# Moving the weights and block sums of a two-layer encoder to multiples of 128 bytes in SBUF

## The chip, the cores and the metric

The kernel runs on one core of one Trainium2 chip. The metric is device time in microseconds from launch to end, as the median of several runs. One execution is also recorded by the hardware profiler; its "page" and the answers of its trace are what this document reads. Engines carry their short names: PE is TensorE's matmul stream, PEld its weight loads, DVE VectorE, ACT ScalarE, POOL GpSimd, SP the engine that issues most transfers.

## The reference

One sequence of 512 frames with 1024 features goes through two layers. Everything is float32.

```python
def reference(x, ...):
    h = x
    for layer in range(2):
        if layer < 1:
            mix = hgrn2_mixer(rms_norm(h, a_norm_pre[0]), a_w_in[0], ...)   # gated recurrence, 8 heads
            h = h + rms_norm(mix, a_norm_post[0])
        else:
            mix = diff_attn_mixer(rms_norm(h, b_norm_pre[0]), k_sh, v_sh, ...)  # 8 heads, two softmaxes each
            h = h + rms_norm(mix, b_norm_post[0])
        ff = squared_relu_mlp(rms_norm(h, mlp_norm_pre[layer]), w_up[layer], w_down[layer])
        h = h + rms_norm(ff, mlp_norm_post[layer])
        if layer == 0:
            k_sh, v_sh = shared_kv(h, kv_norm, w_kv)
    return h
```

Nearly all of the arithmetic is in the projections: the recurrence's input and output projections, the key, value and query projections, the attention's output projection, and in each layer an MLP of 1024 to 4096 to 1024 features.

## The kernel before

**Products in three parts.** TensorE multiplies float32 operands in the type `float32r`, which keeps fewer digits. To keep precision, every operand of a projection is split into a high and a low part: `hi` is the value rounded to float32r, `lo` the rest. A product is then three matmuls (`mm3`, line 224): high by high, high by low, low by high. The high part is written by ScalarE, the low part by VectorE (`split_w` line 166, `split_b` line 195, `split_d` line 185; the activations at lines 389 and 390, 474 and 475).

**Two operands of a matmul.** The stationary operand, 128 by 128, is loaded into the array beforehand (a row LDWEIGHTS on PEld); the moving operand streams through in 128, 256 or 512 columns (a row MATMUL on PE). In `wmm` (line 229) the weights are stationary and the activations moving; in `xmm` (line 235) it is the other way round. All matmuls are issued by the `pe` helper at line 114, so groups of matmuls are told apart by the names of their tiles.

**Tiles.** Activations live feature-major in `xhi` and `xlo` (normed input of a projection) and `uhi` and `ulo` (hidden units or mixer output), four tiles of [128, 2, 512] each, made first, at lines 122 to 127. Weights are fetched in 512 KB pieces into four `raw` buffers by the SP queue (`fetch_w`, line 155) and split into eight `whi` and eight `wlo` buffers in the pool `wp`. The order on TensorE is written out by the program (`Plan`, line 45, with due times); the other engines follow the order in which the program emits, save for chains that get a higher priority.

**Block products.** Quarters 1 to 3 of each MLP's up-projection (`Pair`, line 503) and parts of the gate and value projections (`gates_pair` line 933, `values_pairs` line 974) use seven products of half-size blocks in place of eight. They multiply block sums of the weights (`whi_s`, `whi_t` and their low parts) by block sums of the activations: tiles `t` in the block stage, made by `sums_x` at line 481, and `whi_x` and `wlo_x` in the recurrence, made by `block_sums` at line 702. The accumulators are `ux`, `uy` and `uz`. One product is 12 matmuls of 256 columns. Some of the seven take `t` as the moving operand, the others `xhi` and `xlo`.

**Names in the rows.** `qf`, `g`, `i`: the recurrence's query and forget, gate, and value projections. `ao` and `bo` with `_h` or `_last`: the two mixers' output projections. `up`, `dn`, `dn_h`, `dn_last`: plain up-projection and down-projection. `kq` and `v`: key with query, and value, of the attention. `lg`: attention logits.

**Where tiles start.** The allocator places tiles of the pool `cp` in the order in which they are made, each in a slot rounded up to 32 bytes; `wp` follows, then the pools of the stages (`hg`, `mlp0`, `at`, `mlp1`). `gn` holds 82 gains per partition, 328 bytes, and so takes 352; the same holds for `gnh` (line 144). The addresses of the kernel before, in bytes within a partition:

| tiles | first address | modulo 128 | modulo 512 |
|---|---|---|---|
| xhi, xlo, uhi, ulo (4096 each) | 16512 | 0 | 128 |
| gn (328) | 82048 | 0 | 128 |
| ident, mask, onesd, ones1 | 82400 | 96 | |
| rb (2048) | 84384 | 32 | |
| gnh (328) | 86496 | 96 | |
| raw, whi, wlo (4096 each) | 87488 | 64 | 448 |
| zacc, rs, ss, t, r, u and all other large tiles of the stages | 169408 | 64 | |
| attention's kq, l, at | 192192 | 64 | 192 |

Slices that matmuls take out of x, u, weight and block-sum tiles start at multiples of 512 bytes within the tile, so a row of this table holds for all its slices.

Of the kernel before, what the change touches and what calls it, by code (L numbers as in the profile page):

```python
# [9 lines left out]
F32 = mybir.dt.float32  # L10
# [7 lines left out]
P = 128  # L18
# [23 lines left out]
G_N = 82  # L42
# [46 lines left out]
def trunk_kernel(ctx: ExitStack, tc: tile.TileContext, x_t, w_qf, w_g, w_gs, w_i, w_is, w_ao, w_kv, w_q, w_bo, w_up, w_us, w_dn,  # L89
# [3 lines left out]
    cp = ctx.enter_context(tc.tile_pool(name="cp", bufs=1))  # L93
# [33 lines left out]
    ulo = [cp.tile([P, 2, S], F32R, tag=f"ulo{i}", name=f"ulo{i}", bufs=1) for i in range(4)]  # L127

    res = [x_t.rearrange("(k p) t -> p k t", p=P)[:, :, lo:hi] for lo, hi in ((0, 256), (256, 512))]
    gn = cp.tile([P, G_N], F32, name="gn")  # L130
    a.dma_start(gn, gains)
    ident = cp.tile([P, P], F32, name="ident")
    mask = cp.tile([P, len(LEVELS), 64], U8, name="mask")
# [7 lines left out]
    rcol = cp.tile([P, 4], F32, name="rcol")  # L141
    nrcol = cp.tile([P, 4], F32, name="nrcol")
    ea = rb
    gnh = cp.tile([P, G_N], F32, name="gnh")
    v.tensor_scalar(gnh, gn, -0.5, None, op0=ALU.mult)
    epsc = cp.tile([P, 1], F32, name="epsc")
    v.memset(epsc, EPS)
# [1220 lines left out]
```

## Time and profile before

| | us |
|---|---|
| median of 3 runs | 1262.08 (1261.12 to 1263.5) |
| the profiled execution | 1259.98 |
| its span, first to last instruction | 1258.1 |
| PE busy | 1234.5 |
| PEld busy | 1119.2 |
| DVE busy | 828.9 |
| ACT busy | 669.9 |
| POOL busy | 96.0 |

The mean granted clock of TensorE was 0.997. Matmuls are pipelined: a row's duration runs from a matmul's start to its modelled end and overlaps the next one, so busy time says that TensorE had work, not how fast it went. The chain of work that ended last goes back from the last instruction, step by step, to what released it; its pieces in order of time have a start, a length, an engine, the tile written and the number of instructions merged. By stage: the recurrence layer's mixer runs to about 305 us, its MLP to 652, the attention to about 850 with its output projection to about 900, the second MLP to the end.

### The profile page before, as it was taken

How to read it: one execution, taken by the hardware profiler on the slowest of the kernel's cores; microseconds unless marked ns; L12 is line 12 of the kernel's file. 1: busy time of each engine (PE TensorE's matmuls, PEld its weight loads, DVE VectorE, ACT ScalarE, POOL GpSimd, SP SyncE). 2: the span in 40 equal slices, each digit the busy share in tenths (PEclk: the TensorE clock that was granted, in tenths of full speed). 3: DMA queues.
4: the chain of work that ended last, by engine and by line, in shares of the span. 5: the costliest groups of instructions: out<-in, count | busy, mean ns of one | idle time of the engine just before them, and what ended most of it. 6: DMA issues, size and time to landing. Idle time of an engine off the chain costs nothing.

```text
span 1258.1 us, 21436 instructions
## 1 busy us (share of the span) xinstructions
PE 1234.5 (98%) x8440; PEld 1119.2 (89%) x8440; DVE 828.9 (66%) x1649; ACT 669.9 (53%) x1244; POOL 96.0 (8%) x174
## 2 busy tenths in 40 slices
PE   9999999999999999999999999999999999999996
PEld 7889899999988989989999788889998898988996
DVE  6878887867854735636498978564785473663645
ACT  6454545437742724616456877664773371561732
POOL 0202211110000000000100000001000000000000
PEclk9999999999999999999999999999999999999998
DMA  7224544244366564635526322222435365463522
GB/s 255 90 51 116 112 109 122 88 152 137 105 160 130 169 142 109 182 86 145 191 78 192 115 88 84 85 81 88 152 111 150 93 180 120 114 188 77 162 98 67
DMA packets 56726, 156.44 MB, mean 124 GB/s; under 512 B 6289, under 2 KB 8594, under 8 KB 56626
## 3 DMA queue, kind: packets, MB, share of 16 engines
q1 hardware_dynamic: 45920, 120.34, 30.4%
q0 software_dynamic: 10464, 34.61, 13.0%
q8 instruction: 66, 1.08, 0.3%
q14 instruction: 34, 0.28, 0.1%
q10 hardware_dynamic: 242, 0.13, 0.0%
HBM read 145.35 MB, written 9.70 MB: 123 GB/s over the span
## 4 chain that ended last, share of the span: by engine, by line
PE 87%; DVE 5%; ACT 3%; DMA 3%; issue 2%; POOL 0%; SPq 0%; DVEq 0%; ACTq 0%
PE dn L114 21%; PE ux L114 9%; PE up L114 7%; PE qf L114 7%; PE kq L114 6%; PE dn_h L114 5%; PE uz L114 4%; PE bo_h L114 3%; PE ao_h L114 3%; PE gl L114 3%; PE v L114 2%; PE g L114 2%; PE uy L114 2%; PE i L114 2%; PE lg L114 2%
## 5 line engine op out<-in xcount | busy, mean ns | idle before, releaser
L114 PE MATMUL dn<-uhi,whi_dn 128*128 128x512 f32 x384 | 152.0, 396 | 0.0
L114 PE MATMUL dn<-uhi,wlo_dn 128*128 128x512 f32 x384 | 151.9, 396 | 0.0
L114 PE MATMUL dn<-ulo,whi_dn 128*128 128x512 f32 x384 | 151.8, 395 | 0.0
L114 PEld LDWEIGHTS dn<-uhi,whi_dn 128*128 128x128 f32 x384 | 72.2, 188 | 17.8 <-ACT r L570 0.7
L200 ACT ACTIVATE whi_a<-raw_a 128x1024 fp32r<-128x1024 f32 x24 | 25.4, 1058 | 117.5 <-PE dn L114 114.0
L114 PEld LDWEIGHTS dn<-uhi,wlo_dn 128*128 128x128 f32 x384 | 72.2, 188 | 17.4
L114 PEld LDWEIGHTS dn<-ulo,whi_dn 128*128 128x128 f32 x384 | 72.2, 188 | 16.8
L173 DVE TENSOR_TENSOR wlo_dn<-raw_dn,whi_dn 128x1024 fp32r<-128x1024 f32 x64 | 76.6, 1220 | 5.9 <-ACT whi_dn L172 4.6
L475 DVE TENSOR_TENSOR ulo<-r,uhi 128x1024 fp32r<-128x1024 f32 (+1 forms) x40 | 40.2, 1010 | 53.9 <-ACT uhi L474 53.9
L114 PE MATMUL up<-xhi,wlo_up 128*128 128x256 f32 x256 | 72.1, 281 | 1.0 <-DVE wlo_up L173 1.0
L114 PE MATMUL up<-xhi,whi_up 128*128 128x256 f32 x256 | 72.6, 284 | 0.0
L114 PE MATMUL up<-xlo,whi_up 128*128 128x256 f32 x256 | 71.8, 281 | 0.0
L172 ACT ACTIVATE whi_dn<-raw_dn 128x1024 fp32r<-128x1024 f32 x64 | 65.7, 1051 | 7.2 <-PE up L114 3.0
L114 PE MATMUL dn_h<-uhi,whi_dn 128*128 128x256 f32 x240 | 66.6, 278 | 0.0
L114 PE MATMUL dn_h<-uhi,wlo_dn 128*128 128x256 f32 x240 | 66.3, 276 | 0.0
L114 PE MATMUL dn_h<-ulo,whi_dn 128*128 128x256 f32 x240 | 66.3, 276 | 0.0
L617 DVE TENSOR_TENSOR zacc<-dn,zacc 128x512 f32<-128x512 f32 x32 | 22.1, 691 | 59.1 <-PE dn L114 59.0
L519 POOL DMA_DIRECT2D raw_s<-in_w_us_dram x24 | 20.8, 866 | 488.8 <-DMA raw_s<-in_w_us_dram 301.6
L114 PE MATMUL qf<-xhi,whi_qf 128*128 128x512 f32 x128 | 52.7, 411 | 1.2 <-ACT xhi L686 0.6
L200 ACT ACTIVATE whi_t<-raw_a 128x1024 fp32r<-128x1024 f32 x24 | 25.5, 1061 | 49.4 <-PE dn L114 27.2
L114 PE MATMUL qf<-xlo,whi_qf 128*128 128x512 f32 x128 | 50.7, 396 | 0.3 <-DVE xlo L687 0.3
L114 PE MATMUL qf<-xhi,wlo_qf 128*128 128x512 f32 x128 | 50.7, 396 | 0.0
(533 smaller groups left out, 4124.5 us busy)
## 6 DMA issues: line engine op xcount, KB each, us to landing
raw_dn<-in_w_dn_dram SPq DMA_DIRECT2D x64, 512.0 KB, 4.3
raw_a<-in_w_us_dram SPq DMA_DIRECT2D x24, 512.0 KB, 4.3
raw_s<-in_w_us_dram SPq DMA_DIRECT2D x48, 256.0 KB, 4.3
raw_s<-in_w_us_dram POOLq DMA_DIRECT2D x24, 512.0 KB, 6.4
raw_up<-in_w_up_dram SPq DMA_DIRECT2D x16, 512.0 KB, 4.1
raw_wkv<-in_w_kv_dram SPq DMA_DIRECT2D x16, 512.0 KB, 3.7
raw_qf<-in_w_qf_dram SPq DMA_DIRECT2D x14, 512.0 KB, 4.7
raw_d<-in_w_us_dram SPq DMA_DIRECT2D x12, 512.0 KB, 4.4
```

Of the source, the lines that this page charges most:

```text
L114: nc.tensor.matmul(out, lhsT, rhs, **kw)
L172: last_split[:] = [a.activation(hi, raw, AF.Copy)]
L173: v.tensor_tensor(lo, raw, hi.bitcast(F32), op=ALU.subtract)
L200: a.activation(hi, raw, AF.Copy)
L475: v.tensor_tensor(ulo[pr][:, :, lo:hi], r, uhi[pr][:, :, lo:hi].bitcast(F32), op=ALU.subtract)
L519: g.dma_start(rs, ws[p, :, 0:2, :], accum_op=ALU.add)
L617: v.tensor_tensor(z, pss[n4], z, op=ALU.add)
```

## The change

Two tables of the pool `cp` get 14 more columns than are used. Every instruction sees the same [128, 82] slice as before.

```diff
@@ trunk_kernel
-    gn = cp.tile([P, G_N], F32, name="gn")
+
+    gn = cp.tile([P, G_N + 14], F32, name="gn")[:, :G_N]
     a.dma_start(gn, gains)
     ident = cp.tile([P, P], F32, name="ident")
...
-    gnh = cp.tile([P, G_N], F32, name="gnh")
+    gnh = cp.tile([P, G_N + 14], F32, name="gnh")[:, :G_N]
     v.tensor_scalar(gnh, gn, -0.5, None, op0=ALU.mult)
```

96 columns are 384 bytes, three times 128, in place of a slot of 352. By the allocator's rule each table so moves what follows it by 32 bytes:

| tiles | modulo 128 before | after |
|---|---|---|
| xhi, xlo, uhi, ulo, gn | 0 | 0 |
| ident, mask, onesd, ones1 | 96 | 0 |
| rb | 32 | 64 |
| gnh | 96 | 0 |
| raw, whi, wlo | 64 | 0 |
| large tiles of the stages | 64 | 0 |

The weights and block sums that stood at 448 modulo 512 come to 0 modulo 512; the x and u tiles stay at 128 modulo 512.

## The prediction

> **What bounds the kernel now.** I read the page from the top: span, busy time, granted clock, then the chain of work that ended last.
>
> ```profile
> span 1258.1 us, 21436 instructions
> PE 1234.5 (98%) x8440; PEld 1119.2 (89%) x8440; DVE 828.9 (66%) x1649; ACT 669.9 (53%) x1244; POOL 96.0 (8%) x174
> PEclk9999999999999999999999999999999999999998
> PE 87%; DVE 5%; ACT 3%; DMA 3%; issue 2%; POOL 0%; SPq 0%; DVEq 0%; ACTq 0%
> ```
>
> TensorE is busy for 98% of the span at full clock, and 87% of the chain is TensorE's own work. So the end is set by how far apart matmul starts lie, 8440 times. Everything else is small: DMA, VectorE and ScalarE together hold 11% of the chain, and a few nanoseconds per matmul weigh as much as any stall.
>
> A matmul's duration in the trace includes its run through the array, so it is not the spacing. The spacing is read from long unbroken pieces of the chain in order of time (start, length, what, count): length divided by count.
>
> ```profile
> 36.15 11.00 PE i L114 x48
> 328.12 24.03 PE up L114 x204
> 438.79 44.79 PE dn L114 x192
> 608.20 26.52 PE dn_h L114 x234
> 1080.01 1.44 PE ux L114 x12
> 1081.45 1.38 PE uy L114 x12
> 1082.83 1.36 PE uz L114 x12
> ```
>
> With 512 moving columns: dn 44.79/192 = 233.3 ns, i 11.00/48 = 229.2 ns. With 256: up 117.8, dn_h 113.3, and in the block products of layer 1 ux 120.0, uy 115.0, uz 113.3. Same engine, type and count of columns, up to 6.7 ns apart. The question is whether SBUF addresses make that difference.
>
> By the table of start addresses above, xhi, xlo, uhi and ulo start at 0 modulo 128 and all weights and block sums at 64. I write (moving, stationary). dn, dn_h, up, uy and the uz above are (0, 64). i, with x stationary and weights moving, is (64, 0). The ux piece has block sums t moving over weights: (64, 64), the only kind that sits at 120.
>
> **The change part by part.** No instruction, wait or transfer is added, removed or reordered by the diff. The two paddings move gnh and what follows, as the section on the change lists. For TensorE this means: weights and block sums go from 64 to 0, the x and u tiles stay at 0, so all pairs become (0, 0). The difference between the two operands of dn goes from 64 to 0 modulo 128, while ux keeps a difference of 0 and only its absolute place moves.
>
> *Other engines.* The trace has the same operation with operands at 64 only, and with two of three at 0:
>
> ```profile
> L173 DVE TENSOR_TENSOR wlo_dn<-raw_dn,whi_dn 128x1024 fp32r<-128x1024 f32 x64 | 76.6, 1220 | 5.9 <-ACT whi_dn L172 4.6 <-PE up L114 1.0
> L475 DVE TENSOR_TENSOR ulo<-r,uhi 128x1024 fp32r<-128x1024 f32 x24 | 29.4, 1226 | 46.1 <-ACT uhi L474 46.1
> L172 ACT ACTIVATE whi_dn<-raw_dn 128x1024 fp32r<-128x1024 f32 x64 | 65.7, 1051 | 7.2 <-PE up L114 3.0 <-PE ux L114 2.9 <-PE uz L114 1.3
> L474 ACT ACTIVATE uhi<-r 128x1024 fp32r<-128x1024 f32 x24 | 25.4, 1058 | 0.6
> ```
>
> 1220 against 1226 ns and 1051 against 1058 ns: the operands at 0 are, if anything, 6 ns slower. I take 0 for VectorE and ScalarE. They hold 8% of the chain, about 100 us; 0.6% of that either way is 0.6 us.
>
> *Transfers.* The weights land 64 bytes lower in the 128. Three stalls where TensorE waits for a transfer stand in the chain:
>
> ```profile
> 2.63 7.01 DMA xraw<-in_x_t_dram
> 410.01 7.22 DMA raw_s<-in_w_us_dram
> 579.34 7.29 DMA raw_s<-in_w_us_dram
> ```
>
> The first goes to xraw, which does not move. The others release ux products that wait under 1 us each, since the engine works through most of the 7 us. I take 0; if both stalls vanished it would be about 1 us. [...]
>
> *Block-sum products.* Rows: durations move with the spacing (282 at 120, 277 at 113 to 115).
>
> ```profile
> L114 PE MATMUL ux<-t,whi_t 128*128 128x256 f32 x192 | 35.3, 281 | 0.0
> L114 PE MATMUL ux<-t,wlo_t 128*128 128x256 f32 x96 | 27.1, 282 | 0.0
> L114 PE MATMUL ux<-xhi,wlo_a 128*128 128x256 f32 x96 | 26.6, 277 | 0.0
> L114 PE MATMUL uz<-xhi,wlo_t 128*128 128x256 f32 x96 | 26.5, 276 | 0.0
> ```
>
> Six such groups with t (three of 192, three of 96) make 864 matmuls. Pieces of 12 last 1.42 to 1.44 us, so about 119 ns each; at 113.3 each saves 5.7 ns: 864 x 5.7 = 4.9 us. The x product behind a t product loses 0.02 us to the changeover (1.38 against 1.36); with some 48 of them that is 1.0 us more. From below the term is 0, if it is the difference that counts; I take the whole 5.9 us, the row of the aligned neighbour in the same stage being nearest.
>
> *512 columns.* dn (3 x 384), qf (3 x 128) and kq (6 x 48) are 1824 matmuls at 233.3. The nearest row with stationary operands at 0 is i, at 229.2. Were the place of the stationary operand the cause, all gain 4.1 ns: 7.5 us. Were it not, 0. With one row only, and its moving operand at 64, I take half: 3.7 us.
>
> *256 columns at (0, 64) or (64, 0).* These show two spacings for the same tiles:
>
> ```profile
> 308.22 0.28 PE L114 MATMUL up<-xhi,wlo_up 128*128 128x256 f32 x1
> 309.58 0.28 PE L114 MATMUL up<-xhi,wlo_up 128*128 128x256 f32 x1
> 685.61 0.28 PE L114 MATMUL v<-whi_wkv,xhi 128*128 128x256 f32 x1
> 689.01 0.28 PE L114 MATMUL v<-whi_wkv,xhi 128*128 128x256 f32 x1
> ```
>
> From the first row to the second are 12 starts, 1.36 us: 113.3 ns. Right behind it four matmuls of the norm come in, and the same product goes on at 117.8 (the x204 piece) to its end. From the third to the fourth are 30 starts, 3.40 us: 113.3 again, in a (64, 0) product. So either operand alone may lie at 64 without loss, and how TensorE restarts chooses between the two spacings. New addresses can tip that choice either way: if the 768 of up went to 113.3 it would be 768 x 4.5 = 3.5 us gained; if the 720 of dn_h went the other way, 3.2 us lost. I take 0 and keep both ends.
>
> *Sum.* 5.9 + 3.7 = 9.6 us less. The profiled execution took 1259.98 us (span 1258.1), 2.1 below the median of 1262.08. 1259.98 - 9.6 = 1250.4, and on the median **1252.5 us**.
>
> **The rivals.**
>
> *Forecast: an operand off the 128-byte grid costs TensorE cycles when the other is off it too, and the stationary one costs at 512 columns.* For it: t products against x products in one stage. All terms together give 5.9 + 7.5 + 3.5 = 16.9 us, to 1245; the block-sum term halved and no other gives 1259. Its own range is 1244 to 1259.5.
>
> *Slower: not the place counts but that both operands have the same offset.* TensorE streams the moving operand while it loads the next stationary one; if the two reads collide when they start at the same offset modulo 128, then 64 against 64 collides, 0 against 64 doesn't, and 0 against 0, which this change makes everywhere, does. The rows fit this as well: (64, 64) is slow, both mixed pairs reach 113.3. The only (0, 0) pairs now are a few logits:
>
> ```profile
> L114 PE MATMUL lg<-uhi,ulo 128*128 128x256 f32 x10 | 2.3, 307 | 0.0
> L114 PE MATMUL lg<-kq,kq 128*128 128x256 f32 x6 | 1.2, 282 | 0.0
> L114 PE MATMUL lg<-uhi,ulo 128*128 128x512 f32 x10 | 3.2, 402 | 0.0
> L114 PE MATMUL lg<-kq,kq 128*128 128x512 f32 x6 | 2.0, 410 | 0.0
> ```
>
> lg<-uhi,ulo is (0, 0), lg<-kq,kq is (64, 64): slower at 256 columns (307 against 282), faster at 512 (402 against 410), and both are short bursts between stalls. This is what keeps it open. Price: up 768, dn_h 720, ao_h and bo_h 720, v 384, kq 192 and the x products of the block stage 1152 are 3936 matmuls with a mean spacing near 115. At 118.3 to 120 they lose 3.3 to 5 ns, 13 to 20 us; t products gain nothing. With 512 columns unchanged that is +16.5 us: **1278.6 us**. It decides as soon as more than some 600 of them (2.5 us over 4 ns) go to the slow spacing and the other terms don't come.
>
> *No difference: TensorE's reads don't see addresses of this size.* Then the 120 of ux comes from something else that t products share, and the choice between spacings at restarts falls about as before: **1262 us**, 2.5 either way. [...] The trace doesn't bear it out in full, since ux and uz have the same shape and differ by 6.7 ns; but it can't show that the address is why. That the paddings might not shift the tiles belongs here: table slots are rounded to 32 bytes (328 takes 352), so 384 twice adds 64, and the weights do land on the grid.
>
> **How the numbers follow.** Chances: faster by the forecast's mechanism 0.42, slower by equal offsets 0.34, no difference 0.24. The block-sum rows speak for an effect of addresses; which form it has, the mixed pairs leave almost even. I lean to the forecast for i at 229.2 and for the logits at 512 columns. A measurement of this kernel tells about 0.2%, 2.5 us, from no change. Inside the forecast a little falls within that bound and the no-difference case spreads a little beyond it on both sides, which about cancels: faster 0.42, same 0.23, slower 0.35. The range must hold both signs: 1245 (all terms) to 1279 (the rival near its middle price), which leaves some 0.05 below and 0.12 above.
>
> **What the profile afterwards would show.** Forecast right: ux pieces of 12 at 1.36 to 1.38 us, and dn pieces of 192 near 44 us. Equal offsets: ux stays at 1.44, uz and uy rise to 1.42 or more, dn_h x234 from 26.5 to 27.5 us or more. No difference: all these pieces as they were. Wrong in another way: VectorE or ScalarE groups that change by more than 1%, or a TensorE wait that is new.

## The result and the profile after

| | before | after |
|---|---|---|
| median, us | 1262.42 (4 runs, 1261.12 to 1263.5) | 1269.76 (4 runs, 1268.71 to 1270.5) |
| ratio | | 1.0058 [1.0045, 1.0071] |
| profiled span, us | 1258.1 | 1268.7 |
| mean granted clock | 0.997 | 0.997 |

The kernel became slower by 0.6%: 7.3 us on the medians, 10.6 us between the two profiled spans. The forecast had the sign wrong. The range held the time because it was drawn wide enough for both signs.

The page after, its first part and the shares of the chain of work that ended last:

```profile
span 1268.7 us, 21436 instructions
PE 1247.3 (98%) x8440; PEld 1134.9 (89%) x8440; DVE 828.4 (65%) x1649; ACT 670.5 (53%) x1244; POOL 96.0 (8%) x174
PE 87%; DVE 5%; DMA 3%; ACT 3%; issue 2%; POOL 0%; SPq 0%; DVEq 0%; ACTq 0%
```

The same number of instructions ran on every engine, and the shares of the chain are the same. TensorE's busy time rose by 12.8 us and that of its weight loads by 15.7; VectorE (-0.5) and ScalarE (+0.6) stayed. So, to a percent of the chain, nothing new is waited for: TensorE itself is slower at the same clock.

The chain of the kernel after, pieces in order of time (start, length, what, count):

```profile
36.60 11.14 PE i L114 x48
...
330.13 24.21 PE up L114 x204
...
441.04 44.62 PE dn L114 x192
...
488.52 1.44 PE ux L114 x12
489.96 1.43 PE uy L114 x12
491.39 1.43 PE uz L114 x12
...
611.63 27.77 PE dn_h L114 x234
...
1210.29 27.77 PE dn_h L114 x234
```

Length by count, as in the prediction. With 256 columns: dn_h went from 113.3 to 118.7 ns, up from 117.8 to 118.7, and the three block products, which were 120.0, 115.0 and 113.3, are now all at 119 to 120. With 512 columns dn went the other way, from 233.3 to 232.4, while i rose from 229.2 to 232.1. The loss is spread over the whole run. The x204 piece of up starts 2.0 us later than before (330.13 against 328.12), the first x234 piece of dn_h 3.4 us later (611.63 against 608.20). The second dn_h piece of the kernel before stands here, in its chain:

```profile
1201.67 26.52 PE dn_h L114 x234
```

It starts 8.6 us later after the change, and the end comes 10.6 us later.

Groups of instructions of the kernel after, shapes kept apart (busy us, mean ns of one, idle time before):

```profile
L114 PE MATMUL ux<-t,wlo_t 128*128 128x256 f32 x96 | 27.1, 282 | 0.0
L114 PE MATMUL ux<-xhi,wlo_a 128*128 128x256 f32 x96 | 27.1, 282 | 0.0
L114 PE MATMUL uz<-xhi,wlo_t 128*128 128x256 f32 x96 | 27.0, 281 | 0.0
L174 DVE TENSOR_TENSOR wlo_dn<-raw_dn,whi_dn 128x1024 fp32r<-128x1024 f32 x64 | 76.6, 1221 | 6.3 <-ACT whi_dn L173 5.3 <-PE up L114 1.0
L475 ACT ACTIVATE uhi<-r 128x1024 fp32r<-128x1024 f32 x24 | 25.4, 1057 | 0.6
```

The first row is the one that the change was forecast to speed up: 282 ns before, 282 after. The next two, whose x operand did not move, rose from 277 and 276 to its level. VectorE's and ScalarE's rows are within 1 ns of those before.

### The profile page after: what moved, and what is told of

The parts are those of the page before. It is cut to its first block, busy times and chain, and to the rows that moved or that the text cites. A ratio compares the mean times of both kernels' runs of the same rounds, so it can differ in the third digit from the quotient of the medians.

```text
span 1268.7 us, 21436 instructions
## 1 busy us (share of the span) xinstructions
PE 1247.3 (98%) x8440; PEld 1134.9 (89%) x8440; DVE 828.4 (65%) x1649; ACT 670.5 (53%) x1244; POOL 96.0 (8%) x174
## 4 chain that ended last, share of the span: by engine, by line
PE 87%; DVE 5%; DMA 3%; ACT 3%; issue 2%; POOL 0%; SPq 0%; DVEq 0%; ACTq 0%
PE dn L114 21%; PE ux L114 8%; PE up L114 7%; PE qf L114 6%; PE kq L114 6%; PE dn_h L114 6%; PE uz L114 4%; PE bo_h L114 3%; PE ao_h L114 3%; PE gl L114 3%; PE v L114 3%; DMA raw_s<-in_w_us_dram 2%; PE g L114 2%; PE lg L114 2%; PE i L114 2%
## 5 line engine op out<-in xcount | busy, mean ns | idle before, releaser
L201 ACT ACTIVATE whi_a<-raw_a 128x1024 fp32r<-128x1024 f32 x24 | 25.4, 1059 | 120.2 <-PE dn L114 116.5
```

Of the source, the lines that this page charges most:

```text
L201: a.activation(hi, raw, AF.Copy)
```

## The experiments

For all kernels I worked out one number per family of products from the trace: the mean distance between successive matmul starts, without the pauses, that is distances above 132 ns (256 columns) or 245 ns (512). The second column names d, which turned out to be what matters: the start of the moving operand minus that of the stationary one, in bytes modulo 256, in the kernel before. x stands for the x and u tiles, w for weights and their block sums, t for the block sums of x; "w over x" has weights moving.

```text
ns between starts      d     before after w_only all_64 xw_64 | t_64  w_192 t_112 x_112 xt_112  count
dn, 512, x over w     192     233.3 232.4 232.5  233.3  232.5 | 233.3 227.0 233.3 233.3 233.3   1150
qf, 512, x over w     192     233.2 232.4 232.7  233.3  232.5 | 233.3 228.2 233.3 229.7 230.4    357
i,  512, w over x      64     230.0 231.9 232.5  229.9  232.0 | 230.1 228.6 229.9 232.9 232.9     85
up layer 0            192     117.5 118.7 118.6  117.5  118.6 | 115.9 119.9 117.5 113.8 113.9    380
dn_h layer 0          192     113.4 118.7 118.7  113.4  118.7 | 117.8 120.0 113.4 113.4 113.4    359
dn_h layer 1          192     113.4 118.7 118.7  113.4  118.7 | 113.4 120.0 113.4 113.4 113.4    359
v, w over x            64     116.8 118.7 118.7  116.8  118.6 | 116.8 119.9 116.8 120.0 120.0    373
block, x, layer 0     192     114.5 118.9 118.9  114.5  118.9 | 115.1 120.0 114.2 116.8 113.9    570
block, t, layer 0       0     118.7 119.1 119.1  118.5  119.1 | 116.9 120.0 118.5 119.5 113.6    426
profiled span, us            1258.1 1268.7 1268.4 1258.3 1267.6 | 1259.1 1263.4 1257.7 1259.4 1254.3
```

The two theories at the start are those of the prediction. By **place**, an operand off the 128-byte grid costs time. By **equal offset**, the two reads collide when they start alike. The first four kernels move tiles so that the two part. Their ratios are to 23 runs of the kernel before on the same chip (1260.37 us).

### w_only: weights moved, the small tables not

```diff
-    gnh = cp.tile([P, G_N], F32, name="gnh")
+    gnh = cp.tile([P, G_N + 22], F32, name="gnh")[:, :G_N]
```

gn keeps its slot of 352 bytes and gnh takes 416, so ident, ones1 and rb stay where they were and everything from raw and whi on moves by 64 bytes.

> The second table alone is made 64 bytes longer, so the weights and everything behind them stand where the changed kernel has them (0 modulo 512), while identity, ones, mask and rb keep their old places. Theories that blame the operands of the matmuls (equal offsets modulo 128, or weights that start at a multiple of 128): as the changed kernel, 1269.8 us, dn_h spaced 118.7 ns, dn 232.3. Theory that the moved small tables matter: as before, 1262.4 us, dn_h 113.3, dn 233.3.

Measured: 1269.47 us (5 runs), ratio 1.007 [1.0054, 1.0086]. All spacings are those of the kernel after, to 0.3 ns in most families (i differs by 0.6). The loss comes with the weights and stage tiles; the small tables have no part in it.

### all_64: every large tile moved by 64 bytes

```diff
+    cp.tile([P, 16], F32, name="front")
     xhi = [cp.tile([P, 2, S], F32R, name=f"xhi{i}") for i in range(4)]
```

A tile of 64 bytes ahead of xhi moves x, w and t alike. Weights now stand on the 128-byte grid, as after the change, and x off it; d is as before.

> 64 bytes are put ahead of everything, so x and u tiles go from 0 to 64 modulo 128 and weights and block sums from 64 to 0; the difference of the two operands of every matmul stays as it was before the change. Equal offsets modulo 128 collide: as before, 1262.4 us, dn_h 113.3 ns, up 117.8, dn 233.3, t products 119. Weights at a multiple of 128 are slow in themselves: 1269 to 1270 us, dn_h 118.7 ns.

Measured: 1260.71 us (12 runs), ratio 1.0003 [0.9991, 1.0014]. The chain of this kernel:

```profile
328.37 24.03 PE up L114 x204
...
438.68 44.79 PE dn L114 x192
...
608.36 26.52 PE dn_h L114 x234
```

The lengths of all three pieces equal those of the kernel before to the hundredth of a us. Weights on the grid cost nothing and bring nothing as long as x moves with them. One family, up of layer 1, which the table leaves out, stood at 115.9 ns here and at 117.4 before, though its two operands keep their difference; t_64 below shows that this can happen. The kernel also answers a question on transfers: its weights land at 0 modulo 256, where the kernel before has 192. The group of the largest transfers in the kernel before (count, size, median us from issue to landing):

```profile
raw_dn<-in_w_dn_dram SPq DMA_DIRECT2D x64, 512.0 KB, 4.3
```

The same group in all_64:

```profile
raw_dn<-in_w_dn_dram SPq DMA_DIRECT2D x64, 512.0 KB, 4.5
```

No gain from the address at 0 shows here, in the landing (4.5 us against 4.3) or in the time (1260.71 us against 1260.37).

### xw_64: both moved, with the difference of the kernel after

```diff
+    cp.tile([P, 16], F32, name="front")
     xhi = [cp.tile([P, 2, S], F32R, name=f"xhi{i}") for i in range(4)]
...
-    gnh = cp.tile([P, G_N], F32, name="gnh")
+    gnh = cp.tile([P, G_N + 22], F32, name="gnh")[:, :G_N]
```

x at 64 modulo 128 and w at 64 too: both operands off the grid, their difference as after.

> 64 bytes ahead of everything and 64 more ahead of the weights: x, u, weights and block sums all start at 64 modulo 128, none on the 128-byte grid, and the difference of x and weights is that of the changed kernel. Equal offsets: 1269.8 us, dn_h 118.7 ns, dn 232.3. Weights at a multiple of 128 are slow: as before, 1262.4 us, dn_h 113.3 ns, dn 233.3.

Measured: 1269.33 us (5 runs), ratio 1.0068 [1.0053, 1.0083]. Its chain:

```profile
330.50 24.21 PE up L114 x204
...
441.56 44.62 PE dn L114 x192
...
611.43 27.77 PE dn_h L114 x234
```

These are the lengths of the kernel after, 24.21, 44.62 and 27.77. With all_64 this settles the place for this kernel: the 128-byte grid itself plays no part, neither for one operand (1.0003 with the weights on it and x off) nor for both (1.0068 with both off, 1.007 in w_only with both on). What counts is the difference of the two starts.

### t_64: only the block sums of x moved

```diff
-                    t = pool.tile([P, 2, 4, 256], F32R, tag="big", name=f"t{layer}_{n}", bufs=3)
+                    t = pool.tile([P, 2080], F32R, tag="big", name=f"t{layer}_{n}", bufs=3)[:, 16:2064]
+                    t = t.rearrange("p (a r c) -> p a r c", a=2, r=4)
```

Equal offsets modulo 128 should end for t: its three buffers come to d = 64, 192 and 64.

> The kernel before, with the block sums t of the MLPs alone moved to a multiple of 128 while the weights stay at 64. Equal offsets: the 864 products with t fall from 119 to between 113 and 115 ns, pieces of 12 from 1.42 to 1.44 us to 1.36 to 1.38, and the kernel takes 1256 to 1259 us. Weights at a multiple of 128 are slow, or t products are slow for another reason than their address: unchanged pieces and 1262.4 us.

Measured: 1260.96 us (11 runs), ratio 1.0006 [0.9996, 1.0015]. The t products gained 1.8 ns (118.7 to 116.9), a third of what equal offset promised, and a family that the edit does not touch became slower. The chain of t_64:

```profile
310.68 16.34 PE up L114 x144
327.65 24.03 PE up L114 x204
...
607.74 27.56 PE dn_h L114 x234
...
1202.68 26.52 PE dn_h L114 x234
```

Two pieces of dn_h, with the same addresses, in one execution: 117.8 ns a matmul in layer 0 and 113.3 in layer 1. The two pieces of up differ in the same way: 113.5 and 117.8. So a pair of addresses doesn't have one spacing but can have two. The addresses don't say which one holds; what ran just before is the likely cause, which is argued and not shown. And a difference of 64 is not as good as one of 192, though both are 64 modulo 128: in this run t products right behind other t products, past the change from x, take 117.8 ns.

### probe: every difference in steps of 16 bytes

```diff
+    def probe(wt, x):
+        def group(name, a, b, n, count, rows=P, apart=True):
+            ps = smt(name)
+            if apart:
+                pe.matmul(ps[:, 0:64], onesd, ones1[:, 0:64], start=True, stop=True)
+            for _ in range(count):
+                pe.matmul(ps[:rows, 0:n], wt[:, b:b + rows], x[:, a:a + n], start=True, stop=True)
+        for i in range(16):
+            group(f"pa_{chr(97 + i)}", 4 * i, 0, 256, 24)
+        for i in range(15, -1, -1):
+            group(f"pb_{chr(97 + i)}", 4 * i, 0, 256, 24, apart=False)
+        for i in range(16):
+            group(f"pc_{chr(97 + i)}", 4 * i, 0, 512, 16)
...
```

The kernel before, with some 1400 matmuls put in behind the first head's projection, whose results nobody reads: x slides over a weight tile in steps of 16 bytes. pa has a break between groups, pb runs through all without one in falling order, pc has 512 columns; further groups move both operands (pd) or load fewer columns (pe).

> The kernel before with some 2000 extra matmuls in a row behind the first head's projection, whose results nobody reads: the moving operand starts at x + 16 bytes times a letter, the stationary one at a weight tile; groups pa and pb (256 columns, 24 matmuls, the second time without a break ahead), pc (512 columns, 16), pd (both operands moved), pe (weights of 64 or 32 columns, so a load of half or a quarter). With the weights at 448 and x at 128 modulo 512 the difference is 192 modulo 256 at letter a, 0 at e, 64 at i, 128 at m. Equal offsets modulo 128: pa is slow (118 to 120 ns) at e and m and near 113 at a and i, with the same period in pd whatever the place of the weights, and shorter loads take the loss away. Only the place of one operand counts: pa is flat when the weights stand still, or pd follows the place and not the difference. A kernel time about 250 us longer.

Measured, in one execution, 200 us longer than the kernel before: mean spacing without the first six of a group, ns, by d.

```text
d                0    16    32    48    64    80    96   112   128   144   160   176   192   208   224   240
256 columns  119.8 113.4 117.2 118.4 117.8 119.2 119.9 113.8 118.4 118.6 117.2 119.4 113.4 119.1 118.4 116.9
512 columns  226.7 232.0 233.3 233.6 228.9 231.1 233.3 231.1 233.8 233.3 234.2 233.3 233.3 234.6 233.1 233.3
both moved (256 columns): d = 128: 120.1, 119.0; 192: 117.8, 113.4; 0: 120.0, 119.7; 64: 117.8, 117.8
```

Where the two passes of 256 columns differ (at 0, 32, 80 and 112, by 0.4 to 1.3 ns), their mean stands here; at 16 the first pass gave 113.4 and the second 116.5. Rows behind it from the chain of the probe, of the second pass, with 24 matmuls a piece:

```profile
76.81 2.85 PE pb_m L114 x24
79.66 2.76 PE pb_l L114 x24
82.42 2.88 PE pb_k L114 x24
```

The same chain at 512 columns, a piece being 16 matmuls and two records of the break:

```profile
125.51 3.96 PE pc_d L114 x18
129.47 3.89 PE pc_e L114 x18
```

pb_l (d = 112) takes 2.76 us where its neighbours pb_m (128) and pb_k (96) take 2.85 and 2.88, and all three run on without a break. Leaving out the first six hides something that matters later: after a change of difference the spacing takes a while to settle. In pb_l the distances are 119, 114, 120, 119, 116, 117, 121 and 119 ns before they stay at 113 to 114. At 512 columns the best difference is another one: pc_e (d = 0) is 0.07 us shorter over 16 matmuls than pc_d (d = 240).

Several things follow. For 256 columns only 16, 112 and 192 reach 113.4 to 114; the rest stand at 116.9 to 119.9. Of the three only 112 settled there each time: at 16 the second pass alternated between 114 and 119 to its end. Equal offsets modulo 128 wanted d = 64 near 113; it stood at 117.8. The kernel before stood at one of the three with its x products and came off it: d went from 192 to 128. And 512 columns follow another order, with 0 and 64 in front, so no single offset is best for both. The groups with both operands moved fall on nearly the same values at 0, 64 and 128 (within 1.7 ns), and at 192 on either of two, 117.8 or 113.4. Modulo 256 is enough at the two differences that can be compared: the probe's 128 is 384 modulo 512 while the kernel after stands at 128 there, and the spacings are 118.4 and 118.7; the probe's 0 is 256 modulo 512, and w_192 below, at 0, agrees with it (119.8 and 120.0). A shorter weight load (64 columns in place of 128, which also writes half as many output rows) gave 113.9 at d = 0 and 119.1 at 192, where the full load has 119.8 and 113.4. That speaks for the load taking part in it; more is not shown.

### w_192: weights 192 bytes further, d = 0

```diff
-    gnh = cp.tile([P, G_N], F32, name="gnh")
+    gnh = cp.tile([P, G_N + 54], F32, name="gnh")[:, :G_N]
```

> The weights 192 bytes further than before, so that x minus weights is 0 modulo 256, the slowest place of the probe for 256 columns (120 ns) and its fastest for 512 (226.7 ns). Theory that the difference in steps of 16 bytes sets the spacing, as the probe maps it: dn pieces of 192 fall from 44.8 to 43.5 us, dn_h rises from 113.3 to 120 ns, sum 1824 x 6.6 less and some 3700 x 4.8 more, about 6 us slower than before, 1266 to 1270. Theory that only equal or unequal modulo 128 counts: as the changed kernel in both, dn 232.3, dn_h 118.7, 1270 us. Weights at 128 modulo 512 stand on the 128-byte grid as well.

Measured: 1264.72 us (8 runs), ratio 1.0039 [1.0025, 1.0053]. Its chain:

```profile
440.07 43.60 PE dn L114 x192
...
608.51 28.08 PE dn_h L114 x234
```

dn at 227.0 ns is the fastest of all kernels, dn_h at 120.0 the slowest: at d = 0 the map (226.7 and 119.8) holds in the kernel, in both directions at once. By equal offsets alone dn should have stood at 232.3, as in the kernel after. The time came out below the 1266 to 1270 us expected. Summed over all matmuls of 256 and 512 columns, the distances within the limits rose by 11.2 us and the pauses fell by 5.8, from 87.7 to 81.9; the span rose by 5.3.

### t_112, x_112 and xt_112: one of the good differences

t_112 puts the t buffers at d = 112 and leaves the rest:

```diff
+                    t = pool.tile([P, 2112], F32R, tag="big", name=f"t{layer}_{n}", bufs=3)[:, 28:2076]
+                    t = t.rearrange("p (a r c) -> p a r c", a=2, r=4)
```

x_112 moves the x tiles by 16 bytes and everything behind them (u, w, t) by 96. x over w so comes to 112, w over x to 144; u over w stays at 192 and t over w at 0:

```diff
+    xboth = cp.tile([P, 8216], F32R, name="xboth")[:, 4:8196].rearrange("p (i a b) -> p i a b", a=2, b=S)
+    xhi = [xboth[:, i] for i in range(4)]
+    xlo = [xboth[:, 4 + i] for i in range(4)]
```

xt_112 has both edits.

> The kernel before, with the block sums t of the MLPs at 112 bytes modulo 256 behind the weights, the place where the probe fell to 113.4 ns in both passes. By the map: t products from 119 to 113.5 ns, and since the x products behind them keep their own place, 1255 to 1258 us; if restarts tip the x products to 117.8 as in the run with 64 bytes, no gain, 1261. Equal or unequal modulo 128 alone: like the run with 64 bytes, t at 117.4.

> The kernel before, with xhi and xlo as slices of one tile, placed 112 bytes modulo 256 behind the weights; u stays at 192 and t at 0. By the map: up from 117.8 to 113.5 ns and the x products of the block stage from 115 to 113.5, qf and kq from 233.3 to 231.1; together 3.4 + 1.7 + 1.5 us less, 1254 to 1257 us. If the probe's map doesn't carry over to the kernel's triples: 1262 us or more.

> Both of the last two edits: x and t products all at 112 bytes modulo 256. By the map 5 to 12 us under the kernel before, 1249 to 1256 us, with pieces of 12 in the block stage at 1.36 to 1.37 us whatever their operand. If the two spacings at a place are chosen by restarts alone: some stages at 117.8 and 1258 to 1262 us.

Measured, on one chip with 25 runs of the kernel before (1260.21 us):

| | us | ratio |
|---|---|---|
| t_112 (10 runs) | 1258.9 | 0.999 [0.9978, 1.0002] |
| x_112 (10 runs) | 1260.59 | 1.0005 [0.9995, 1.0016] |
| xt_112 (7 runs) | 1255.51 | 0.9959 [0.9946, 0.9972] |

Neither edit alone does anything that can be told from no change, so the forecasts by the map for these two (1255 to 1258 and 1254 to 1257 us) missed. Together the edits make the kernel 0.41% faster than before and so faster than both kernels of this study. Pieces of the chain of x_112:

```profile
328.53 23.15 PE up L114 x204
...
402.42 1.42 PE uy L114 x12
```

And of the chain of xt_112:

```profile
328.58 23.18 PE up L114 x204
...
400.98 1.36 PE ux L114 x12
402.34 1.36 PE uy L114 x12
403.70 1.36 PE uz L114 x12
405.06 2.72 PE ux L114 x24
```

up, away from t products, gains in both: 113.5 ns against 117.8. In the block stage the pieces of xt_112 are all at 113.3. In x_112 the uy piece, an x product at d = 112 behind a t product at 0, still takes 1.42 us. Pieces of the chain of t_112:

```profile
485.54 1.40 PE uz L114 x12
486.94 1.36 PE ux L114 x12
...
493.83 1.43 PE uz L114 x12
```

All three are t products at d = 112. The second follows another t product and takes 113.3 ns a matmul; the first and the third follow x products at 192. The distances of the third, from the timeline of t_112, are 126, 130, 119, 118, 114, 120, 119, 116, 118, 120, 120 and 113 ns: the spacing settles as in the probe's pb_l, and the product of 12 is over when it has. So the mean of 118.5 for the t products of t_112 is the price of the change from one difference to another and not of the place 112. Whole products of 12 without a pause, by what ran just ahead, mean ns:

```text
               before  t_112  x_112  xt_112
t behind x      118.5  119.1  119.5   113.3
t behind t      120.0  113.3  120.0   113.3
x behind t      114.9  113.9  118.3   113.3
x behind x      113.3  113.9  113.3   113.3
```

The block stage changes between x and t at nearly every product. It gains only when both stand at the same good difference, where there is nothing to settle.

The map is good to about 2 ns. v in x_112, at d = 144, stands at 120.0 where the probe has 118.6; dn in the kernel after, at 128, at 232.4 where the probe has 233.8; i in w_192, at 0, at 228.6 where the probe has 226.7.

The spacings of xt_112 alone would give about 8 us (t 853 x 5.1 ns, up 760 x 3.6, qf and kq some 600 x 2.7, x of the block stage 1140 x 0.6, against v 373 x 3.2 lost). The span fell by 3.8. The rest went into pauses. Waits of TensorE's weight loads in the kernel before (total us, times, longest):

```profile
PEld ux L114 <- DVE r L565: 2.2, 5, 0.7
...
PEld gl L114 <- issue: 1.4, 4, 0.4
```

The same waits in xt_112:

```profile
PEld ux L114 <- DVE r L567: 3.4, 5, 1.1
...
PEld gl L114 <- issue: 2.2, 4, 1.3
```

These two add 2.0 us. That a faster TensorE reaches its inputs sooner is my reading of it. The whole shows in the same two sums as for w_192, with the signs reversed: the distances within the limits fell by 9.6 us and the pauses rose by 5.9, from 87.7 to 93.6, which together is the change of the span.

## Why the prediction was wrong

**What bounds the kernel** held: the end follows the distance between matmuls, and the changes of span in this study follow from it once the pauses are counted.

**Other engines** and **Transfers** (taken 0) held: VectorE and ScalarE moved by -0.5 and +0.6 us of busy time, DMA keeps 3% of the chain, and all_64 shows no gain from the landing address (4.5 us from issue to landing against 4.3, ratio 1.0003).

**Block-sum products** (-5.9 us) failed. The 864 t products were to go from 119 to 113.3 because their operands came onto the grid; they went from 118.7 to 119.1. (Behind another t product, a t product of 12 stood at 120.0 before and after; the mean is lower because of those behind an x product, at 118.5 and 119.0.) The step compared t products at (64, 64) with x products at (0, 64) and took the cheaper row as the price of the aligned state. That row was no aligned neighbour: it stood at another difference, 192, one of the three good ones. The changeover term (1.0 us) didn't come either: the uy piece lengthened from 1.38 to 1.43.

**256 columns at (0, 64) or (64, 0)** was the step that cost most. It was taken at 0 with ends 3.5 us apart on either side, on the ground that either operand alone may lie at 64 without loss. The rows showed that; they did not show that the loss stays away when the other operand comes to the same offset. Measured: some 3700 of x over w went from a mean of 115.0 to 118.7 ns, 13.7 us, and some 440 with weights moving from 116.9 to 118.6, 0.8 us. The part of the step on two spacings was right: t_64 shows the same product with the same addresses at 117.8 and 113.3 in one execution.

**512 columns** (-3.7 us) had the right sign and was mis-sized: dn, qf and kq gained 0.8 to 1.4 ns, not the 2.05 taken, about 1.7 us in all, and i, from which the figure came, lost 1.9. For i the map gives the reason: it stood at d = 64 (228.9 in the probe), not at a better place of its stationary operand. The small gain of dn it doesn't give (233.3 at 192, 233.8 at 128), so the sign of this term was right for a cause that no run shows.

Sum by measured spacings: 13.7 + 0.8 + 0.4 (t) - 1.7 = 13.2 us; the span rose by 10.6. Counted over all matmuls of 256 and 512 columns, the distances within the limits rose by 14.1 us and the pauses fell by 3.4, from 87.7 to 84.3, which closes the sum. That a slower TensorE reaches its inputs later, and so waits less, is my reading of it.

**The rivals.** "Slower: the same offset" named the right sign, the right family and, at the low end, the price of the spacings: 13 to 20 us over 3936 matmuls against 13.7 over 3700. Its time, 1278.6 us, was too long by 9. Its marks (uy at 1.43, dn_h at 27.77) came as written. As a rule it fell: 64 and 192 are alike modulo 128 and differ by 4.4 ns, 16 and 112 can be as good as 192, and at 512 columns d = 0 is the fastest. The rule that fits all nine runs, to about 2 ns, is finer: the difference modulo 256, in steps of 16 bytes, together with the settling after each change and the two spacings at 192. "No difference" fell with the ratio of 1.0058, and with the probe: starts of the same matmul of 256 columns lie 113.4 ns apart at d = 192 and 119.8 at d = 0, so for this type of operand the address of one matters to the other. Where that happens no run shows.

The deeper fault lay in the notation. Writing each pair as two places modulo 128 made 64 and 192 one class, and rows that differ in d were read as if they differed in place. The logits, which the prediction leaned on for the forecast, run in fours of mixed shapes between other products, too few in a row to show a spacing, and carried nothing.

What stays open: which part of the chip makes the two operands disturb each other, what picks one of the two spacings at 192, and why dn gained 0.9 ns. The runs show when it happens, not why.

## What to carry to other kernels

Where TensorE's own pace sets the end, the start addresses of the two operands of a matmul are a parameter like a tile size (in this kernel they were worth 0.58% one way and 0.41% the other): read the distance between starts family by family, and compare differences of addresses, not places on a grid. Moving one table by a few bytes moves every tile behind it, so a change of that kind is worth a look at the unbroken pieces before and after. When a stage mixes short products, put all of them at one good difference, since after a change the spacing took eight matmuls (pb_l of the probe) to a dozen (t_112) to settle. A sum of spacings is not yet a time: count the pauses too, which gave back 3 to 6 us here.

## What the runs showed of the hardware

- Back-to-back float32r matmuls of 256 columns, loads of 128, at a mean granted clock of 0.998: 113.4 to 120.1 ns apart by the difference of the operand starts; 512 columns: 226.7 to 234.6 (probe). The same tiles on the grid or off it made no difference (all_64 1.0003, xw_64 1.0068 like w_only 1.007).
- After a change of the difference the spacing took eight matmuls (pb_l) to a dozen (t_112) to settle at a good one: at d = 112 a product of 12 took 119.1 ns a matmul behind one at 192 and 113.3 behind one at 112 (t_112).
- One pair of addresses held either of two spacings, each for a whole piece of 234 matmuls: at d = 192, 113.3 and 117.8 ns (dn_h in t_64).
- The kernel before spread more than w_192 on the same chip: 25 runs from 1256.0 to 1262.73 us against 8 from 1264.05 to 1265.26. Whether the two spacings at 192 are the reason no run shows.
